# Strassen products for two row units in twelve gate/up pairs, silu as one ScalarE function, and another order in the first output pair

## The chip, the core and the metric

The kernel runs on one core of one Trainium2 chip. The metric is the device time of one execution in microseconds (us); less is better. A core has five engines with instruction queues of their own: TensorE (PE, with its weight loads as PEld), VectorE (DVE), ScalarE (ACT), GpSimd (POOL) and SyncE (SP), which here only issues DMAs. They wait for each other through semaphores.

## The reference, cut to what matters

Two layers of a decoder trunk on x of 256 rows by 2048 channels, all in float32. The part that this change bears on:

```python
for l in range(DEPTH):                       # 2
    h = rms_norm(x, mix_norm[l])
    proj = h @ w_in[l]                       # 2048 x 7680: q, k, v, u, v of the gating unit, two gates
    ...                                      # window attention, spatial gating, two branch projections
    merged = gates[..., :D_MODEL] * branch_a + gates[..., D_MODEL:] * branch_b
    x = x + merged @ w_out[l]                # 2048 x 2048
    h2 = rms_norm(x, ffn_norm[l])
    x = x + (jax.nn.silu(h2 @ w_gate[l]) * (h2 @ w_up[l])) @ w_down[l]   # 2048 x 5632, twice, and 5632 x 2048
```

## The kernel before, in words

**Products.** Every large matrix product is cut into weight tiles of 256 rows by 512 columns (a "half", 512 KB). A float32 weight tile `raw` is split into a high part `whi` (ScalarE, a copy to fp32r, line 228) and a low part `wlo = raw - whi` (VectorE, line 229); the activations, transposed, are kept as `uh` and `ul` in the same manner. One product of 128 rows of x with such a tile is six matmuls of 512 columns (`add_product`, lines 316 to 325): for each of two 128-row parts high by high, low by high, high by low. A "unit" is 512 channels of the activations, so two halves.

**The list of entries.** `plans` holds the work in order; a plan is one column block (`single`) or two column blocks that are worked together (`pair`): gate and up block f of the feed-forward part (key "ffn"), two blocks of w_out ("mix"), two of w_down ("hid"), two of w_in ("in"). All plans are flattened to one list `entries`. An entry with tag X, G or U takes one weight tile and both row blocks of x: two products. The entries with tags P1 to P7 are the seven products of a Strassen scheme (Winograd's form) over one unit and both column blocks, one product each, where the plain way takes four entries of two products. They need four weight tiles (k11, k12, k21, k22), four differences of them, made in place on VectorE (`sums`, line 213), four combinations of the activations (`sh`, `sl`, made by `sums` and `finished` in `transposed`, lines 467 to 482), and two results that are kept aside and given back (`kept`, lines 346 to 352). One unit of a pair is done so (unit `WINO` = 0); the others are plain. The first six entries of a pair (the head: P1, P5, P2, P6, P7, P4) are interleaved with the last six entries of the plan before, so that TensorE has plain work while ScalarE and VectorE copy between them; P3 stands in the body, behind the pair's third G entry.

**What runs ahead.** `Stream.next` is called once an entry: it asks for the weight DMAs of entries up to `W_LOAD` = 7 ahead (all on SP's queue), splits up to `W_SPLIT` = 4 ahead (four buffers each for `whi` and `wlo`, so that the split of entry n+4 waits until TensorE has done entry n), and makes the differences up to `W_SUM` = 6 ahead. Plain weight tiles rotate through five buffers; k11 to k22 have one each.

**Ticks.** Work that is not a weight split is queued with `after(n, fn)`, and `tick` counts once for every two products. `transposed` turns 512 channels by VectorE block transposes and 16 small DMAs (`turn`, lines 386 to 399; on POOL's queue, or half on SP's with `queue=None`), then makes the parts some ticks later; the tuples `WINO_...` give the ticks of the six steps for a unit that a Strassen scheme needs. With `on_pe` TensorE transposes instead (line 436).

**Order around the change.** In a layer: projections, attention and gating, the two branches with the gates (lines 933 to 952), two "mix" pairs with the residual (`residual`, line 867 on; the norm of the feed-forward part is made there), then three rounds of feed-forward: gate/up pairs 0 to 3, two "hid" pairs, pairs 4 to 7, two "hid" pairs, pairs 8 to 10, two "hid" pairs. `hidden` (line 961 on) makes one 512-channel block of the hidden layer: `on_gate` runs when the last G entry is done, `on_up` when the pair is done. Silu is made as x/2 times (1 + tanh(x/2)), with rhalf = r/2 and rr = r*r/2 from the norm: a ScalarE tanh (line 967), a VectorE product (line 968), and `on_up`'s product (line 972). The order on TensorE is that of the program; on the other engines a scheduler orders the instructions ahead of the launch.

Of the kernel before, what the change touches and what calls it, by code (L numbers as in the profile page):

```python
# [8 lines left out]
F32 = mybir.dt.float32  # L9
# [5 lines left out]
P = 128  # L15
# [42 lines left out]
def hybrid_trunk(ctx: ExitStack, tc: tile.TileContext, x, mix_norm, w_in, q_norm, k_norm, sinks,  # L58
# [62 lines left out]

        return Plan(key, [], [half(w, h, "X") for h in range(w.shape[0] // (2 * P))])

    def pair(key, wa, wb, by_unit=False):

        h1, h2 = 2 * WINO, 2 * WINO + 1
        l11, l12, l21, l22 = (load_of(w, h, t) for w, h, t in ((wa, h1, "k11"), (wb, h1, "k12"), (wa, h2, "k21"),  # L130
                                                              (wb, h2, "k22")))
        k11, k12, k21, k22 = l11[0], l12[0], l21[0], l22[0]
        rest = [h for h in range(wa.shape[0] // (2 * P)) if h // 2 != WINO]
        g, u = [half(wa, h, "G") for h in rest], [half(wb, h, "U") for h in rest]
        head = [dict(tag="P1", loads=[l11, l12], src=k11),
                dict(tag="P5", loads=[], sums=[(k11, k12, k11)], src=k11),
                dict(tag="P2", loads=[l21, l22], src=k21),
                dict(tag="P6", loads=[], sums=[(k11, k22, k11)], src=k11),
                dict(tag="P7", loads=[], sums=[(k12, k22, k12)], src=k12),
                dict(tag="P4", loads=[], sums=[(k21, k21, k11)], src=k21)]  # L140
        p3 = dict(tag="P3", loads=[], src=k22)
        body = g[:2] + [g[2], p3] + g[3:] + u
        g[1]["then"] = "open"
        if by_unit:
            body = g[:2] + [p3] + u[:2]
            g[0]["then"] = g[1].pop("then")
            for i in range(2, len(rest), 2):
                body += g[i:i + 2] + u[i:i + 2]
        return Plan(key, head, body)

    plans = []
    for l in range(DEPTH):
        wl = w_in[l]

        def of_in(kind, c):
            o = {"kv": O_KV, "q": 0, "v": O_V, "u": O_U, "gate": O_GATE}[kind] + c * CW
            return wl[:, o:o + CW]

        for f in FIRST_PART[l]:
            plans.append((single if len(f) == 1 else pair)(("in", l), *(of_in(*c) for c in f)))  # L160
        plans += [single(("att", l), w) for w in cols_of(w_attn_branch[l], NCH)]
        sgu = [single(("sgu", l), w_sgu_branch[l, :, j * CW:(j + 1) * CW]) for j in range(NCH)]
        plans += [sgu[0], pair(("in", l), of_in("gate", 5), of_in("gate", 6)), sgu[1], sgu[2],
                  single(("in", l), of_in("gate", 7)), sgu[3]]
        c_ = cols_of(w_out[l], NCH)
        plans += [pair(("mix", l), c_[j], c_[j + 1]) for j in range(0, NCH, 2)]
        for r, (f0, f1) in enumerate(ROUNDS):
            for f in range(f0, f1):
                plans.append(pair(("ffn", l), w_gate[l, :, f * CW:(f + 1) * CW], w_up[l, :, f * CW:(f + 1) * CW], f == 0))
            c_ = cols_of(w_down[l, f0 * CW:f1 * CW, :], NCH)  # L170
            plans += [pair(("hid", l, r), c_[j], c_[j + 1], j == 0) for j in range(0, NCH, 2)]
    entries = []
    for p in plans:
        if p.head:
            h, n = p.head, min(6, len(ahead.body))
            t = [entries.pop() for _ in range(n)][::-1]
            if n == 6:
# [3 lines left out]
            ahead_of = order[order.index(h[3]) - 1]  # L181
            ahead_of["loads"] = ahead_of["loads"] + h[2].pop("loads")
            h[2]["loads"] = []
            entries += order
        entries += p.body
        ahead = p

    class Stream:
# [7 lines left out]
        def load(self, upto):  # L196
            while self.asked < min(upto, len(entries)):
                for key, w, h, tag in entries[self.asked]["loads"]:
                    raw = wraw.tile([P, 2, CW], F32, tag=tag, name=nm("raw"), bufs=None if tag == "raw" else 1)
# [127 lines left out]
    def step():  # L327
# [4 lines left out]
        if tag in "XGU":  # L332
            ps = banks(p, "b" if tag == "U" else "a")
            todo = [(ps[t], block(units, e["h"], t)) for t in range(NT)]
        else:
            sh, sl = units[WINO][2:]
            which, t, form = {"P1": ("a", 1, (0, 0)), "P2": ("a", 0, (1, 0)), "P6": ("a", 1, 1), "P7": ("a", 1, 2),
                              "P4": ("a", 1, (1, 1)), "P5": ("a", 0, 0), "P3": ("b", 0, 3)}[tag]
            todo = [(banks(p, which)[t], (sh[:, form], sl[:, form]) if isinstance(form, int)
                     else block(units, 2 * WINO + form[0], form[1]))]  # L340
        for ps, u in todo:
            add_product(p, ps, u, w, tag in ("P4", "P7"))
        a, b = p.acc.get("a"), p.acc.get("b")
        if tag == "P5":
            p.kept = slot([P, 2, CW], name="kept")
            nc.scalar.activation(p.kept[:, 1, :], a[0], AF.Copy)
            nc.scalar.activation(a[0], a[1], AF.Copy)
        elif tag in ("P6", "P7"):
            nc.vector.tensor_tensor(out=p.kept[:, int(tag == "P7"), :], in0=a[1], in1=p.kept[:, 1, :], op=ALU.add)  # L349
# [144 lines left out]
    class Norm:  # L494
# [13 lines left out]
        def unit(self, c, on_pe=False, again=False, queue=nc.gpsimd, late=0):  # L508
            transposed(self.units, c, xs[:, :, c * CW:(c + 1) * CW], cols=self.cols[:, 4 * c:4 * c + 4],
                       on_pe=on_pe, again=again, queue=queue, late=late,  # L510
                       wino=None if c != WINO or on_pe else WINO_FIRST if again else WINO_IN if self.soon else
                       WINO_NORM)

        def finish(self):
            self.r, self.rh, self.rr = [], [], []
            for t in range(NT):
                v = tiny(1, f"var{t}", 2)
                nc.vector.tensor_reduce(out=v, in_=self.ss[t], axis=AX.X, op=ALU.add)
# [5 lines left out]
                rr = tiny(1, f"rr{t}", 2)  # L524
                nc.vector.tensor_tensor(out=rr, in0=r_, in1=rh, op=ALU.mult)
                self.r.append(r_)
                self.rh.append(rh)
                self.rr.append(rr)

    norm = Norm(first_cols)  # L530
    units_at["in", 0] = norm.units
# [335 lines left out]
    def residual(key, nxt=None, scale=1.0, store=False):  # L867

        def chunk(j, sums):
# [25 lines left out]
    for l in range(DEPTH):  # L895
# [43 lines left out]
        for j in range(NCH):  # L939
# [6 lines left out]
            for t in range(NT):  # L946
                nc.vector.scalar_tensor_tensor(out=gb[:, t, :], in0=gb[:, t, :], scalar=1.0, in1=ps[t],
                                               op0=ALU.add, op1=ALU.mult)
                nc.vector.tensor_tensor(out=ga[:, t, :], in0=ga[:, t, :], in1=gb[:, t, :], op=ALU.add)
# [11 lines left out]
        def hidden(hT, c):  # L961
            hid = slot([P, NT, CW], name="hid")

            def on_gate(g):
                for t in range(NT):
                    th = hid[:, t, :]
                    nc.scalar.activation(th, g[t], AF.Tanh, scale=norm.rh[t])  # L967
                    nc.vector.scalar_tensor_tensor(out=th, in0=th, scalar=1.0, in1=g[t], op0=ALU.add, op1=ALU.mult)  # L968

            def on_up(up):  # L970
                for t in range(NT):
                    nc.vector.scalar_tensor_tensor(out=hid[:, t, :], in0=up[t], scalar=norm.rr[t], in1=hid[:, t, :],
                                                   op0=ALU.mult, op1=ALU.mult)
                pe, soon = c == len(hT) - 1 == 2, c == 3
                after(3 if pe else 1 if soon else 2,
# [54 lines left out]
```

## Time and profile before

| what | us |
|---|---|
| median of 3 runs (2469.06 to 2469.82) | 2469.17 |
| the profiled execution's own time | 2468.67 |
| its span (first to last instruction) | 2467.0 |
| TensorE clock granted, mean | 0.999 |
| ScalarE busy / VectorE busy in the span | 1431.0 / 1932.5 |

The profiled execution's time is 1.67 us over its span, and 0.5 us under the median. A busy TensorE says only that matmuls followed each other; what one costs is read from the distance of their starts.

### The profile page before, as it was taken

What the parts mean: (1) busy time and instruction counts of PE and PEld (TensorE: products, weight loads), DVE (VectorE), ACT (ScalarE), POOL (GpSimd) and SP (SyncE); (2) the same over time, 40 slices, a digit from 0 to 9 for tenths busy, and PEclk for the clock granted to TensorE, in tenths of its full rate; (3) what the DMA queues carried; (4) which work ended last, traced back from release to release, by engine and by line L of the source; (5) the groups of instructions that cost most, each with busy time, mean ns of one, the idle gap of its engine ahead of it and who ended that gap; (6) DMA issues with size and microseconds to landing.
All of it is one profiled execution on the core that took longest, in us unless ns stands there. A gap on an engine that the chain in (4) does not pass through costs nothing.

```text
span 2467.0 us, 31322 instructions
## 1 busy us (share of the span) xinstructions
PE 2452.7 (99%) x11040; PEld 2027.6 (82%) x11040; DVE 1932.5 (78%) x2274; ACT 1431.0 (58%) x1793; POOL 309.3 (13%) x576
## 2 busy tenths in 40 slices
PE   9999999999999999999999999999999999999999
PEld 7888888888888888888887888888888888888887
DVE  6798676888877787778887986767888777877786
ACT  5567544565655565556655665455656555655564
POOL 3100002232110111001101000022311101110110
PEclk9999999999999999999999999999999999999999
DMA  9555667676666667576747446676767666666664
GB/s 293 199 187 162 214 197 220 184 235 205 216 210 202 216 193 234 180 225 190 225 153 265 154 154 225 205 213 182 236 198 233 200 216 195 219 207 203 215 195 146
DMA packets 279502, 505.69 MB, mean 205 GB/s; under 512 B 27760, under 2 KB 39120, under 8 KB 279344
## 3 DMA queue, kind: packets, MB, share of 16 engines
q1 hardware_dynamic: 261776, 485.83, 61.7%
q0 software_dynamic: 17248, 17.59, 2.7%
q8 instruction: 86, 1.41, 0.2%
q14 instruction: 72, 0.59, 0.1%
q10 hardware_dynamic: 320, 0.27, 0.0%
HBM read 475.27 MB, written 2.10 MB: 194 GB/s over the span
## 4 chain that ended last, share of the span: by engine, by line
PE 95%; DMA 2%; DVE 2%; SPq 1%; ACT 0%; issue 0%; POOL 0%; DVEq 0%; ACTq 0%
PE acc L324 61%; PE acc L325 31%; DMA raw<-in_w_in_dram 2%; DVE wlo L229 1%; PE po L780 1%; SPq L399 1%; PE psc L741 0%; PE ppt L770 0%; PE pt L436 0%; ACT whi L228 0%; PE psg L858 0%; POOL rq L296 0%; DVE box L393 0%; DVE ul L427 0%; DVE raw L213 0%
## 5 line engine op out<-in xcount | busy, mean ns | idle before, releaser
L229 DVE TENSOR_TENSOR wlo<-raw,whi 128x1024 fp32r<-128x1024 f32 (+1 forms) x1039 | 1261.8, 1220 | 478.8 <-ACT whi L228 465.7
L228 ACT ACTIVATE whi<-raw 128x1024 fp32r<-128x1024 f32 (+1 forms) x1038 | 1097.6, 1059 | 908.5 <-PE acc L325 709.9
L324 PE MATMUL acc<-whi,uh 128*128 128x512 f32 x3114 | 1216.6, 391 | 0.9 <-ACT uh L422 0.9
L324 PE MATMUL acc<-wlo,uh 128*128 128x512 f32 x3114 | 1213.3, 390 | 1.8 <-DVE wlo L229 1.8
L325 PE MATMUL acc<-whi,ul 128*128 128x512 f32 x3114 | 1212.8, 389 | 0.0
L324 PEld LDWEIGHTS acc<-wlo,uh 128*128 128x128 f32 x3114 | 585.2, 188 | 124.7 <-DVE wlo L229 4.2
L325 PEld LDWEIGHTS acc<-whi,ul 128*128 128x128 f32 x3114 | 585.0, 188 | 122.4 <-DVE ul L427 0.5
L324 PEld LDWEIGHTS acc<-whi,uh 128*128 128x128 f32 x3114 | 585.0, 188 | 121.7 <-ACT uh L422 1.1
L399 POOL DMA_DIRECT2D tt<-box x528 | 259.6, 499 | 1710.2 <-DMA raw<-in_w_up_dram 503.6
L213 DVE TENSOR_TENSOR raw<-raw,raw 128x1024 f32<-128x1024 f32 x188 | 229.4, 1220 | 1.3
L324 PE MATMUL acc<-whi,sh 128*128 128x512 f32 x376 | 147.2, 391 | 0.0
L324 PE MATMUL acc<-wlo,sh 128*128 128x512 f32 x376 | 146.9, 391 | 0.0
L325 PE MATMUL acc<-whi,sl 128*128 128x512 f32 x376 | 146.4, 389 | 0.0
L325 PEld LDWEIGHTS acc<-whi,sl 128*128 128x128 f32 x376 | 70.6, 188 | 14.8
L324 PEld LDWEIGHTS acc<-wlo,sh 128*128 128x128 f32 x376 | 70.6, 188 | 14.7 <-DVE kept L349 0.4
L324 PEld LDWEIGHTS acc<-whi,sh 128*128 128x128 f32 x376 | 70.6, 188 | 14.3
L349 DVE TENSOR_TENSOR kept<-acc,kept 128x512 f32<-128x512 f32 x94 | 64.3, 684 | 0.0
L352 ACT ACTIVATE acc<-kept 128x512 f32<-128x512 f32 x94 | 55.0, 586 | 11.0 <-DVE kept L349 10.9
L875 DVE SCALAR_TENSOR_TENSOR xs<-acc,xs 128x512 f32<-128x512 f32 (+1 forms) x66 | 41.4, 667 | 7.8 <-PE acc L325 7.8
L967 ACT ACTIVATE hid<-acc,rhalf 128x512 f32<-128x512 f32 x44 | 30.4, 690 | 20.7 <-PE acc L325 20.7
L419 DVE TENSOR_TENSOR ul<-tt,uh 128x512 fp32r<-128x512 f32 x52 | 34.0, 685 | 2.9 <-ACT uh L418 2.9
L968 DVE SCALAR_TENSOR_TENSOR hid<-hid,acc 128x512 f32<-128x512 f32 x44 | 29.6, 684 | 8.3 <-ACT hid L967 8.3
(137 smaller groups left out, 874.9 us busy)
## 6 DMA issues: line engine op xcount, KB each, us to landing
raw<-in_w_in_dram SPq DMA_DIRECT2D x239, 512.0 KB, 4.8
raw<-in_w_up_dram SPq DMA_DIRECT2D x176, 512.0 KB, 5.0
raw<-in_w_gate_dram SPq DMA_DIRECT2D x176, 512.0 KB, 4.3
raw<-in_w_down_dram SPq DMA_DIRECT2D x176, 512.0 KB, 5.0
raw<-in_w_out_dram SPq DMA_DIRECT2D x64, 512.0 KB, 5.1
tt<-box POOLq DMA_DIRECT2D x528, 32.0 KB, 4.4
raw<-in_w_attn_branch_dram SPq DMA_DIRECT2D x32, 512.0 KB, 5.5
raw<-in_w_sgu_branch_dram SPq DMA_DIRECT2D x32, 512.0 KB, 4.4
```

Of the source, the lines that this page charges most:

```text
L213: self.last = nc.vector.tensor_tensor(out=self.raws[d], in0=self.raws[x], in1=self.raws[y], op=ALU.subtract)
L228: self.high = nc.scalar.activation(hi[:, i, :], raw[:, i, :], AF.Copy)
L229: self.last = nc.vector.tensor_tensor(out=lo[:, i, :], in0=raw[:, i, :], in1=hi[:, i, :].bitcast(F32), op=ALU.subtract)
L324: nc.tensor.matmul(ps, a, part[:, kk, :], start=first and kk + n == 0, stop=False, skip_group_check=True)
L325: nc.tensor.matmul(ps, b, hi[:, kk, :], start=False, stop=kk == 1, skip_group_check=True)
L349: nc.vector.tensor_tensor(out=p.kept[:, int(tag == "P7"), :], in0=a[1], in1=p.kept[:, 1, :], op=ALU.add)
L352: nc.scalar.activation(ps, p.kept[:, t, :], AF.Copy)
L399: q.dma_start(dst[j * B:(j + 1) * B, i], box[i * B:(i + 1) * B, j])
L419: nc.vector.tensor_tensor(out=l, in0=s_, in1=h.bitcast(F32), op=ALU.subtract)
L875: nc.vector.scalar_tensor_tensor(out=xs[:, t, sl], in0=sums[t][:, i * w:(i + 1) * w], scalar=scale, in1=xs[:, t, sl], op0=ALU.mult, op1=AL ...
L967: nc.scalar.activation(th, g[t], AF.Tanh, scale=norm.rh[t])
L968: nc.vector.scalar_tensor_tensor(out=th, in0=th, scalar=1.0, in1=g[t], op0=ALU.add, op1=ALU.mult)
```

## The change

**Two units share banks.** `pair(..., two=True)` does units 0 and 1 by Strassen products: the products of both units with the same tag go to the same PSUM bank one after the other, and only behind the second one are results kept, copied or given back (`done`). It is used in the gate/up pairs 4, 5, 6, 8, 9 and 10 of each layer, twelve in all. Such a pair has a head of twelve entries, two P3 in the body, and four G and four U entries. The head is interleaved with nine entries of the plan before instead of six. Between two such pairs one period of the entry list then is (a and b are units 0 and 1; g and u are entries of two products, P of one):

```
g0 g1 P1a P1b g2 P3a P5a P5b P3b g3 P6a P6b P2a P2b u0 u1 P7a P7b u2 u3 P4a P4b
```

where g, u and P3 belong to one pair and the other P to the next. The loads of unit 1's four weight tiles take a slot of the general pool (25 buffers of 4 KB a partition) instead of buffers of their own, and those of both P2 are asked for with P5.

**Preparing unit 1.** Its four combinations are made once a layer, 24 ticks behind the last "mix" chunk, by a second call of `transposed` for that unit (again two block transposes, 16 DMAs, scaled copies, four sums, a split).

**Silu.** One ScalarE function `Silu` takes the place of tanh; the VectorE product of line 968 falls away, and `on_up` multiplies by r. `rr` is no longer made.

**First output pair.** With `last_later` its last two G entries stand behind the first two U entries; the last gate chunk is transposed one tick later; the ticks of the norm's unit 0 are two earlier, and its 16 DMAs go half by SP, half by POOL.

```diff
-WINO_NORM = 7, 8, 10, 11, 12, 13
+WINO_NORM = 5, 6, 8, 9, 10, 11
+W_TWO = 24
@@ pair
+        both = (WINO, WINO + 1) if two else (WINO,)
+        for w in both:
+            h1, h2 = 2 * w, 2 * w + 1
+            l11, l12, l21, l22 = (load_of(m, h, t if w == WINO else "slot")
+                                  for m, h, t in ((wa, h1, "k11"), (wb, h1, "k12"), (wa, h2, "k21"), (wb, h2, "k22")))
...
+            for e in head[-1] + p3[-1:]:
+                e["unit"], e["done"] = w, w == both[-1]
+        head = [e for es in zip(*head) for e in es]
...
-        body = g[:2] + [g[2], p3] + g[3:] + u
+        body = g[:3] + p3 + g[3:] + u
+        if last_later:
+            body = g[:3] + p3 + g[3:4] + u[:2] + g[4:] + u[2:]
@@ plans
-        plans += [pair(("mix", l), c_[j], c_[j + 1]) for j in range(0, NCH, 2)]
+        plans += [pair(("mix", l), c_[j], c_[j + 1], last_later=j == 0) for j in range(0, NCH, 2)]
+                                  two=r > 0 and f - f0 < 3))
@@ entries
-            h, n = p.head, min(6, len(ahead.body))
+            h, n = p.head, min(6 if len(p.head) == 6 else 9, len(ahead.body))
+            if n == 9:
+                order = t[:1] + h[:2] + t[1:3] + h[2:4] + t[3:5] + h[6:8] + h[4:6] + t[5:7] + h[8:10] + t[7:9] + h[10:]
+                for i in range(2):
+                    h[2 + i]["loads"], h[4 + i]["loads"] = h[4 + i]["loads"], []
@@ step
-        if tag == "P5":
+        if not e.get("done", True):
+            pass
+        elif tag == "P5":
@@ residual
-                after(1 if last else 2, lambda: nxt.unit(j, j > 0 and nxt.soon, queue=None if last else nc.gpsimd,
+                after(1 if last else 2, lambda: nxt.unit(j, j > 0 and nxt.soon, queue=None if last or j == WINO and not nxt.soon else nc.gpsimd,
+                    if not nxt.soon:
+                        after(W_TWO, lambda: nxt.unit(WINO + 1, again=True))
@@ gates
-            after(2 + (j == NCH - 1), lambda j=j, ga=ga: transposed(mT, j, ga, on_pe=j == NCH - 1,
+            after(2 + 2 * (j == NCH - 1), lambda j=j, ga=ga: transposed(mT, j, ga, on_pe=j == NCH - 1,
@@ hidden
-                    th = hid[:, t, :]
-                    nc.scalar.activation(th, g[t], AF.Tanh, scale=norm.rh[t])
-                    nc.vector.scalar_tensor_tensor(out=th, in0=th, scalar=1.0, in1=g[t], op0=ALU.add, op1=ALU.mult)
+                    nc.scalar.activation(hid[:, t, :], g[t], AF.Silu, scale=norm.r[t])
...
-                    nc.vector.scalar_tensor_tensor(out=hid[:, t, :], in0=up[t], scalar=norm.rr[t], in1=hid[:, t, :],
+                    nc.vector.scalar_tensor_tensor(out=hid[:, t, :], in0=up[t], scalar=norm.r[t], in1=hid[:, t, :],
```

More of the change, by code (lines that the diff above doesn't have):

```diff
@@ L122, in single, with pair @@
         return Plan(key, [], [half(w, h, "X") for h in range(w.shape[0] // (2 * P))])
[L124 to L133, printed above, removed]
-        g, u = [half(wa, h, "G") for h in rest], [half(wb, h, "U") for h in rest]
[L135 to L141, printed above, removed]
-        body = g[:2] + [g[2], p3] + g[3:] + u
+    def pair(key, wa, wb, by_unit=False, last_later=False, two=False):
+        head, p3 = [], []
+        both = (WINO, WINO + 1) if two else (WINO,)
[3 more added lines that the diff above has]
+                                  for m, h, t in ((wa, h1, "k11"), (wb, h1, "k12"), (wa, h2, "k21"), (wb, h2, "k22")))
+            k11, k12, k21, k22 = l11[0], l12[0], l21[0], l22[0]
+            head.append([dict(tag="P1", loads=[l11, l12], src=k11),
+                         dict(tag="P5", loads=[], sums=[(k11, k12, k11)], src=k11),
+                         dict(tag="P2", loads=[l21, l22], src=k21),
+                         dict(tag="P6", loads=[], sums=[(k11, k22, k11)], src=k11),
+                         dict(tag="P7", loads=[], sums=[(k12, k22, k12)], src=k12),
+                         dict(tag="P4", loads=[], sums=[(k21, k21, k11)], src=k21)])
+            p3.append(dict(tag="P3", loads=[], src=k22))
+            for e in head[-1] + p3[-1:]:
+                e["unit"], e["done"] = w, w == both[-1]
+        head = [e for es in zip(*head) for e in es]
+        rest = [h for h in range(wa.shape[0] // (2 * P)) if h // 2 not in both]
+        g, u = [half(wa, h, "G") for h in rest], [half(wb, h, "U") for h in rest]
+        body = g[:3] + p3 + g[3:] + u
@@ L180, in hybrid_trunk @@
                 order = [h[0], t[0], h[1], t[1], h[3], h[2], t[2], h[4], t[3], h[5]]
-            ahead_of = order[order.index(h[3]) - 1]
-            ahead_of["loads"] = ahead_of["loads"] + h[2].pop("loads")
-            h[2]["loads"] = []
+            if n != 9:
+                ahead_of = order[order.index(h[3]) - 1]
+                ahead_of["loads"] = ahead_of["loads"] + h[2]["loads"]
+                h[2]["loads"] = []
             entries += order
@@ L198, in load @@
                 for key, w, h, tag in entries[self.asked]["loads"]:
-                    raw = wraw.tile([P, 2, CW], F32, tag=tag, name=nm("raw"), bufs=None if tag == "raw" else 1)
+                    raw = (slot([P, 2, CW], name="raw") if tag == "slot" else
+                           wraw.tile([P, 2, CW], F32, tag=tag, name=nm("raw"), bufs=None if tag == "raw" else 1))
                     src = w[2 * h * P:2 * (h + 1) * P, :].rearrange("(k p) n -> p k n", p=P)
@@ L335, in step @@
         else:
-            sh, sl = units[WINO][2:]
             which, t, form = {"P1": ("a", 1, (0, 0)), "P2": ("a", 0, (1, 0)), "P6": ("a", 1, 1), "P7": ("a", 1, 2),
                               "P4": ("a", 1, (1, 1)), "P5": ("a", 0, 0), "P3": ("b", 0, 3)}[tag]
-            todo = [(banks(p, which)[t], (sh[:, form], sl[:, form]) if isinstance(form, int)
-                     else block(units, 2 * WINO + form[0], form[1]))]
+            todo = [(banks(p, which)[t], tuple(x[:, form] for x in units[e["unit"]][2:]) if isinstance(form, int)
+                     else block(units, 2 * e["unit"] + form[0], form[1]))]
         for ps, u in todo:
```

14 lines of the change are left out of this document (5 added, 9 removed).

## Prediction

> **What bounds the kernel now.** I read the page first, then the costliest groups, the waits and a stretch of the timeline.
>
> ```profile
> span 2467.0 us, 31322 instructions
> PE 2452.7 (99%) x11040; PEld 2027.6 (82%) x11040; DVE 1932.5 (78%) x2274; ACT 1431.0 (58%) x1793; POOL 309.3 (13%) x576
> PEclk9999999999999999999999999999999999999999
> PE 95%; DMA 2%; DVE 2%; SPq 1%; ACT 0%; issue 0%; POOL 0%; DVEq 0%; ACTq 0%
> ```
>
> The fourth line is the chain that ended last: 95% of it is TensorE, at full clock. So time falls if TensorE gets fewer matmuls, and rises where somebody lets it wait. The price of a matmul is the distance of starts, not the recorded 390 ns (they overlap). Six matmuls, one product, lie between these two rows of the timeline:
>
> ```profile
> 605.07 0.39 PE L324 MATMUL acc<-whi,uh 128*128 128x512 f32 x1
> 606.43 0.39 PE L324 MATMUL acc<-whi,uh 128*128 128x512 f32 x1
> ```
>
> One product is 1.36 us, a matmul 0.2267. The waits say who has kept TensorE, and what limits the engines that feed it:
>
> ```profile
> PE pt L436 <- DVE gate L949: 2.9, 2, 1.4
> PE acc L324 <- DVE wlo L229: 1.8, 5, 0.6
> ACT whi L228 <- PE acc L325: 709.9, 646, 4.4
> DVE wlo L229 <- ACT whi L228: 465.7, 486, 7.8
> ```
>
> (total us, times, longest.) TensorE waited 2.9 us for the transposes of the last gate chunk and 1.8 for low parts. The feeders wait in a ring: ScalarE for a buffer that TensorE must free, VectorE for ScalarE. They have slack, VectorE less.
>
> **The change part by part.**
>
> *Twelve units by seven products instead of eight.* One product saved in each of 12 pairs (2 layers, rounds of blocks 4 to 6 and 8 to 10): 12 x 1.36 = **16.3 us** off TensorE, since the granted clock and the form of the matmuls stay. Nothing is added on TensorE; results of both units are copied and kept once.
>
> *The gate chunk's transposes one tick later.* A tick is two products, 2.72 us, the wait is 1.4 each of two times; and last_later puts two U entries ahead of the G entries that read this chunk, 5.44 us. **-2.9 us**. What is late next is those G entries; behind the transposes stand P3, g3 and the two U entries, 9.5 us, for four short copies.
>
> *What the second unit costs its feeders.* Rows by form (busy us, mean ns):
>
> ```profile
> L229 DVE TENSOR_TENSOR wlo<-raw,whi 128x1024 fp32r<-128x1024 f32 x1035 | 1259.1, 1222 | 478.8 <-ACT whi L228 465.7 <-DMA raw<-in_w_up_dram 3.0 <-DMA tt<-box 1.5
> L213 DVE TENSOR_TENSOR raw<-raw,raw 128x1024 f32<-128x1024 f32 x188 | 229.4, 1220 | 1.3
> L349 DVE TENSOR_TENSOR kept<-acc,kept 128x512 f32<-128x512 f32 x94 | 64.3, 684 | 0.0
> L972 DVE SCALAR_TENSOR_TENSOR hid<-acc,rr,hid 128x512 f32<-128x512 f32 x44 | 30.9, 744 | 0.0
> L968 DVE SCALAR_TENSOR_TENSOR hid<-hid,acc 128x512 f32<-128x512 f32 x44 | 29.6, 684 | 8.3 <-ACT hid L967 8.3
> L393 DVE STREAM_TRANSPOSE box<-hid 128x512 f32<-128x512 f32 x40 | 28.2, 704 | 0.0
> L228 ACT ACTIVATE whi<-raw 128x1024 fp32r<-128x1024 f32 x1035 | 1095.8, 1060 | 908.5 <-PE acc L325 709.9 <-DVE raw L213 54.5 <-issue 52.5
> L967 ACT ACTIVATE hid<-acc,rhalf 128x512 f32<-128x512 f32 x44 | 30.4, 690 | 20.7 <-PE acc L325 20.7
> L467 ACT ACTIVATE sh<-sums 128x1024 fp32r<-128x1024 f32 x12 | 12.6, 1046 | 0.5 <-DVE sums L482 0.5
> L463 ACT ACTIVATE flat<-tt 128x256 f32<-128x256 f32 x32 | 10.6, 401 | 0.0
> L468 DVE TENSOR_TENSOR sl<-sums,sh 128x1024 fp32r<-128x1024 f32 x12 | 14.6, 1218 | 0.0
> L482 DVE TENSOR_TENSOR sums<-flat 128x256 f32<-128x256 f32 x24 | 10.0, 419 | 0.0
> ```
>
> Back to back, VectorE starts the next operation before the recorded end of the last:
>
> ```profile
> 1044.28 1.23 DVE L229 TENSOR_TENSOR wlo<-raw,whi 128x1024 fp32r<-128x1024 f32 x1 [1.46 <-ACT whi L228]
> 1045.42 1.22 DVE L213 TENSOR_TENSOR raw<-raw,raw 128x1024 f32<-128x1024 f32 x1
> 1046.56 0.68 DVE L349 TENSOR_TENSOR kept<-acc,kept 128x512 f32<-128x512 f32 x1
> 1047.16 2.35 DVE L229 TENSOR_TENSOR wlo<-raw,whi 128x1024 fp32r<-128x1024 f32 x2
> 1050.91 0.69 DVE L349 TENSOR_TENSOR kept<-acc,kept 128x512 f32<-128x512 f32 x1
> ```
>
> A 1024-wide one occupies 1.14 us, a 512-wide one 0.60. Between two two-unit pairs a period has 22 entries and 30 products, 40.8 us of TensorE. VectorE has 22 low parts and 8 differences, 30 x 1.14 = 34.2; two kept sums 1.2; two up products, 744 ns each and so some 0.66 apart, 1.3: 36.7. Such periods are 4 to 5 and 8 to 9 (call them A), and 5 to 6 and 9 to 10 (B), in two layers: eight in all. B has also the two block transposes of the round's first block, 1.3: 38.0. So VectorE is filled to 90 and 93%: no loss over the period, but its freedom is gone. Before, a period was 31 products, 42.2 us, with 23 x 1.14 + 1.2 + 1.2 (the product of L968) + 1.3 and, at most, some 2.5 for a hidden block: 32.4, 77%.
>
> Now the order inside. A high part starts 0.2 us after TensorE has freed the buffer of the entry four before (row below: 605.27 against 605.07), takes 1.06, the low part 1.14 more.
>
> ```profile
> 605.27 1.06 ACT L228 ACTIVATE whi<-raw 128x1024 fp32r<-128x1024 f32 x1 [1.66 <-PE acc L325]
> 606.63 0.69 ACT L967 ACTIVATE hid<-acc,rhalf 128x512 f32<-128x512 f32 x1 [0.30 <-PE acc L325]
> 607.99 0.69 ACT L967 ACTIVATE hid<-acc,rhalf 128x512 f32<-128x512 f32 x1 [0.67 <-PE acc L325]
> 608.58 1.05 ACT L228 ACTIVATE whi<-raw 128x1024 fp32r<-128x1024 f32 x1
> ```
>
> Counting from the start of g0, with each difference two entries ahead of its split, I get the low part of g3 at 15.6 us and TensorE there at 16.3; P6a 17.9 against 19.0, P6b 19.0 against 20.4, P2a 20.7 against 21.8. At g3's end ScalarE must wait for both banks for Silu (the rows at 606.63 and 607.99), so the high part of P2b runs from 20.1 to 21.1, its low part to 22.2, against 23.1. In B the scaled copies of the first hidden block (2 x 401 ns, some 0.65 together) come in there too: 0.3 to 0.5 us are left. Then u0 23.4 against 24.5, u1 26.2 against 27.2, P7a 28.9 against 29.9. Nothing is late, nothing by much more than 1 us in time. Bounds: nothing, to 1 us of stall in each of the eight, 8 us; nearest row is the 1.8 us that low parts cost all of before, so I take 0.2 each, **+1.6 us**.
>
> *Weights.* In such a period 11 of 16 tiles (5.8 MB) are asked for in some 14 us, 420 GB/s. The chip moved this much in two stretches:
>
> ```profile
> 10.00:30.00 20.00, 19.87 (x93) 16.19 (x92) 11.79 (x26) 13.16 (x29) 4.88 (x9) 0.92 1.05 373
> 295.00:305.00 10.00, 10.00 (x45) 8.27 (x45) 6.33 (x6) 5.75 (x7) 0.00 (x0) 1.00 1.04 388
> raw<-in_w_up_dram SPq DMA_DIRECT2D x176, 512.0 KB, 5.0
> ```
>
> (the last column of the first two is GB/s; the third is a tile's median us to landing.) At 388 they take 14.9, one us more than asked. k11 comes free with P4a's difference at about 32 us and must be back for the next high part at 39.4: 5.0 fits. I take 0; one of 512 KB late would cost about its 1.35 us of transfer, 8 times 11 at most in the eight.
>
> *The hidden block ahead of the last "hid" pairs.* The steps of a round's first hidden block are due at fixed ticks, and pair 10 is shorter in front of the next head: its P5 stood five products behind the last step (sh, sl) and now directly behind it, with g3's Silu in between. ScalarE needs 1.05, VectorE 1.14 more. If the scheduler puts sh ahead of the Silus, 0.7 us are lost; between them, 1.2; behind both, 2.9. I take 1.0 in each of two layers, **+2.0 us**; bounds 0 and 5.8.
>
> *Preparing unit 1.* Per layer on VectorE 2 x 0.70 + 4 x 0.42 + 1.22 = 4.3 us, on ScalarE 4 x 0.40 + 1.05 = 2.7, 16 small DMAs on POOL. It falls into round 0, whose stretch has 31 us of idle VectorE and 72 of ScalarE in 175, and POOL's queue 147:
>
> ```profile
> 585.00:760.00 175.00, 175.00 (x774) 144.96 (x773) 144.08 (x161) 103.08 (x115) 27.58 (x56) 1.00 0.69 218
> ```
>
> Cost 0; with that cover gone 2 x 7.0 = 14 us.
>
> *Silu.* The product of L968 goes (29.6 us), from an engine that has idled: 0 on the path, at most the 1.8 us above. The function itself I price as the tanh row, 690 ns. It may need another table:
>
> ```profile
> L272 ACT ACT_TABLE_LOAD x1 | 1.3, 1283 | 1.3 <-PEq L1008 1.3
> ```
>
> One load served copy, square, tanh and exp. If Silu lies elsewhere, three loads are added (into layer 0's feed-forward, out of it, into layer 1's): 3.85 us of ScalarE. Two meet wide entries with slack, the third the crowded start of layer 1. Bounds 0 and 3.85, I take half a load, **+0.6 us**. [...]
>
> *Order of the first output pair.* The last G two entries later and the ticks two earlier cancel: unit 0 of the norm is ready as before. Eight DMAs move to SP, ahead of weight loads. The chain has such an issue with its price:
>
> ```profile
> 109.70 0.59 SPq L399
> ```
>
> 8 x 0.59 = 4.7 us of SP, twice. Loads are asked for far enough ahead (five plain buffers, some 11 us less the 5.0 to landing); the same split is used before for the last chunk, and TensorE never waited there. 0; without the cover 9.4.
>
> **The sum.** -16.3 - 2.9 + 1.6 + 2.0 + 0.6 = -15.0. From the profiled execution's 2468.67 that is 2453.7; the median of before stands 0.5 above it, so **2454.2**.
>
> **The rivals.** *No stall at all:* 2468.67 - 19.2 + 0.5 = 2450.0. For it: TensorE waited 1.8 us for low parts in the whole of before. Faster as well.
>
> *The feeders eat it:* 1 us in each of eight periods, 2.9 in each of two layers and 3.85 for tables: 8 + 5.8 + 3.9 = 17.7 against 19.2, so 2467.7: within 0.2%. For it speaks B's slack of 0.3 us, against it the same row.
>
> *Table loads around each Silu:* if copy weren't in Silu's table, 88 loads, 113 us of ScalarE. A pair would have 2.6 us more in front of P2b; less the slack of about 1 that is 8 x 1.6 = 12.8, 2466 to 2467. Against it: copy, square, tanh and exp share one load. [...]
>
> *Slower: difference, high part and low part run one after the other.* In a head each product needs a difference (VectorE), then a high part (ScalarE), then a low part (VectorE). Were VectorE idle for the 1.06 us of each of the eight, a period would need 36.7 + 8.5 = 45.2 in A and 46.5 in B, against 40.8: 4.4 and 5.7 lost, four times each, 40 us; with the sum above less its 1.6, 2492.5. It decides from 3.0 us a period (24.1 / 8). Against it: the rows from 1044.28 to 1051.5, a head now, show VectorE waiting 0.3 us; for it, 12 one-product entries in a period instead of six or seven, and VectorE at 90%.
>
> **How the numbers follow.** About 0.2% (4.9 us) is what a measurement can tell from no change. Forecast 0.56, no stall 0.30, feeders 0.04, tables 0.02, serial 0.08. Faster 0.86, same 0.06, slower 0.08. The range goes from 2449.0 (no stall, and something of the 1.8 us) to 2465.0, where the stalls of the heads, of P5 and the tables are near their upper ends.
>
> **What would show it.** Matmuls of 512 columns fall by 72. The gate wait on L436 is gone. The waits of TensorE for wlo, sh and sl tell the 1.6 and the 2.0; they should stand at P2b in B and at the P5 behind pair 10. VectorE's share in A and B is 90% or more. Table loads are four. I am wrong if TensorE waits over 1 us in most of the eight heads, or for weight DMAs, or if loads stand beside each Silu.

## The result, and the profile after

The changed kernel takes 2457.38 us (median of 6 runs, 2456.94 to 2459.4), the kernel before 2469.11 beside it: ratio 0.9949, 95% interval 0.9939 to 0.9958, so 11.7 us less (10.4 to 15.1 by the interval) where 15.0 were forecast. The profiled execution took 2457.45 us, its span is 2455.7. From the page, as before:

```profile
span 2455.7 us, 31363 instructions
PE 2438.1 (99%) x10968; PEld 2012.6 (82%) x10968; DVE 1999.5 (81%) x2320; ACT 1472.5 (60%) x1842; POOL 315.6 (13%) x592
PE 90%; DVE 3%; DMA 3%; SPq 1%; issue 1%; ACT 1%; DVEq 0%; ACTq 0%
```

Matmuls fall from 11040 to 10968, the 72 that were counted. VectorE has 67 us more to do, ScalarE 42. In the last line, the chain that ended last, TensorE has fallen from 95% to 90%: the chain passes through the other engines more often. That is no measure of what was lost; TensorE's own waits are 13.5 us in all, 10.0 before. These lead (total us, times, longest):

```profile
PE acc L341 <- DVE sl L485: 3.2, 2, 1.6
PE acc L340 <- DVE wlo L245: 2.9, 5, 0.8
PE ppt L783 <- DVE wsT L654: 2.4, 1, 2.4
PE acc L340 <- ACT acc L364: 1.7, 1, 1.7
```

The wait for the gate chunk is gone. Two waits are new: for sl, twice (the low part of unit 0's combinations for the last "hid" pairs), and for the ScalarE copy that moves the kept banks (line 364), once.

The eight tight periods are not among them. Here are layer 0's: windows of 40.8 us that hold period A and B of round 1, then of round 2 (length; busy us and count of TensorE, weight loads, VectorE, ScalarE, POOL; granted clock, busy share of the DMA engines, GB/s):

```profile
806.50:847.30 40.80, 40.80 (x181) 33.78 (x180) 37.19 (x35) 25.38 (x28) 0.00 (x0) 1.00 0.56 180
847.30:888.10 40.80, 40.80 (x181) 33.78 (x180) 38.47 (x37) 27.78 (x34) 7.84 (x16) 1.00 0.61 192
1055.80:1096.60 40.80, 40.80 (x181) 33.78 (x180) 37.19 (x35) 25.38 (x28) 0.00 (x0) 1.00 0.55 179
1096.60:1137.40 40.80, 40.80 (x181) 33.56 (x180) 37.87 (x37) 27.63 (x34) 7.86 (x16) 1.00 0.63 192
```

Each holds 180 matmuls in 40.8 us, 0.2267 apiece (the 181st lies across an edge): TensorE loses nothing while VectorE is busy for 91 to 94%.

The loss is just behind them, where the head of the last "hid" pairs begins. TensorE, then VectorE, from the timeline:

```profile
1153.22 0.40 PE L340 MATMUL acc<-wlo,sh 128*128 128x512 f32 x1
1155.19 0.50 PE L341 MATMUL acc<-whi,sl 128*128 128x512 f32 x1 [1.58 <-DVE sl L485]
```

```profile
1151.31 0.42 DVE L499 TENSOR_TENSOR sums<-flat,sums 128x256 f32<-128x256 f32 x1
1151.65 1.22 DVE L245 TENSOR_TENSOR wlo<-raw,whi 128x1024 fp32r<-128x1024 f32 x1
1152.78 1.22 DVE L229 TENSOR_TENSOR raw<-raw,raw 128x1024 f32<-128x1024 f32 x1
1153.92 1.22 DVE L485 TENSOR_TENSOR sl<-sums,sh 128x1024 fp32r<-128x1024 f32 x1
```

P5's third matmul is due 0.23 us behind the second and starts 1.97 behind it. With the smaller delays around it the place costs 2.1 us, in both layers. The last sum of the combination ends at 1151.7, and a low part and a difference for later weights stand between it and sl. In layer 1 a second stall follows, at P6. ScalarE's timeline there:

```profile
2381.04 1.06 ACT L244 ACTIVATE whi<-raw 128x1024 fp32r<-128x1024 f32 x1 [1.67 <-PE acc L341]
2382.01 1.13 ACT L435 ACTIVATE uh<-tt 128x512 fp32r<-128x512 f32 x2
2383.05 0.57 ACT L363 ACTIVATE kept<-acc 128x512 f32<-128x512 f32 x1
2383.76 1.06 ACT L244 ACTIVATE whi<-raw 128x1024 fp32r<-128x1024 f32 x1
2384.73 0.58 ACT L364 ACTIVATE acc<-acc 128x512 f32<-128x512 f32 x1
```

P5 has been done since about 2378.3, but its two copies (lines 363 and 364) stand behind a high part that waits for a later entry, behind two parts of another hidden block and behind one more high part. P6 has to wait for the second copy until 2385.3.

### The profile page after: what moved, and what is told of

Its sections match the earlier page's. It is cut to its first block, busy times and chain, and to the rows that moved or that the text cites. A ratio compares the mean times of both kernels' runs of the same rounds, so it can differ in the third digit from the quotient of the medians.

```text
span 2455.7 us, 31363 instructions
## 1 busy us (share of the span) xinstructions
PE 2438.1 (99%) x10968; PEld 2012.6 (82%) x10968; DVE 1999.5 (81%) x2320; ACT 1472.5 (60%) x1842; POOL 315.6 (13%) x592
## 4 chain that ended last, share of the span: by engine, by line
PE 90%; DVE 3%; DMA 3%; SPq 1%; issue 1%; ACT 1%; DVEq 0%; ACTq 0%
PE acc L340 59%; PE acc L341 29%; DMA raw<-in_w_in_dram 2%; DVE wlo L245 2%; SPq L416 1%; ACT whi L244 1%; PE po L793 1%; PE psc L754 0%; PE ppt L783 0%; DVE raw L229 0%; PE psg L871 0%; PE pt L453 0%; DMA raw<-in_w_up_dram 0%; DMA raw<-in_w_down_dram 0%; DVE box L410 0%
## 5 line engine op out<-in xcount | busy, mean ns | idle before, releaser
L244 ACT ACTIVATE whi<-raw 128x1024 fp32r<-128x1024 f32 (+1 forms) x1074 | 1132.0, 1059 | 883.0 <-PE acc L341 623.4
L245 DVE TENSOR_TENSOR wlo<-raw,whi 128x1024 fp32r<-128x1024 f32 (+1 forms) x1075 | 1301.3, 1219 | 399.0 <-ACT whi L244 386.7
L340 PE MATMUL acc<-whi,uh 128*128 128x512 f32 x2994 | 1170.3, 391 | 1.2 <-ACT uh L439 1.2
L340 PE MATMUL acc<-wlo,uh 128*128 128x512 f32 x2994 | 1167.1, 390 | 3.0 <-DVE wlo L245 2.9
L341 PE MATMUL acc<-whi,ul 128*128 128x512 f32 x2994 | 1166.4, 390 | 0.0
L229 DVE TENSOR_TENSOR raw<-raw,raw 128x1024 f32<-128x1024 f32 x236 | 287.8, 1219 | 1.6 <-DMA raw<-in_w_up_dram 0.8
L341 PE MATMUL acc<-whi,sl 128*128 128x512 f32 x472 | 184.0, 390 | 3.2 <-DVE sl L485 3.2
L340 PE MATMUL acc<-whi,sh 128*128 128x512 f32 x472 | 184.8, 392 | 1.7 <-ACT acc L364 1.7
L340 PE MATMUL acc<-wlo,sh 128*128 128x512 f32 x472 | 184.2, 390 | 0.0
L435 ACT ACTIVATE uh<-tt 128x512 fp32r<-128x512 f32 x52 | 29.8, 618 | 9.4 <-DMA tt<-box 9.4
```

Of the source, the lines that this page charges most:

```text
L229: self.last = nc.vector.tensor_tensor(out=self.raws[d], in0=self.raws[x], in1=self.raws[y], op=ALU.subtract)
L244: self.high = nc.scalar.activation(hi[:, i, :], raw[:, i, :], AF.Copy)
L245: self.last = nc.vector.tensor_tensor(out=lo[:, i, :], in0=raw[:, i, :], in1=hi[:, i, :].bitcast(F32), op=ALU.subtract)
L340: nc.tensor.matmul(ps, a, part[:, kk, :], start=first and kk + n == 0, stop=False, skip_group_check=True)
L341: nc.tensor.matmul(ps, b, hi[:, kk, :], start=False, stop=kk == 1, skip_group_check=True)
L435: nc.scalar.activation(h, s_, AF.Copy)
```

## The experiments

Twelve kernels were run, each with the kernel before on the same chip. "Stretch" below is what the distances between neighbouring 512-wide matmuls have over 0.2267 us in the profiled execution, summed where it is more than 15 ns: 10.9 us before, 19.6 after. The waits are always TensorE's.

**One part alone.** First the order of the first output pair, without the rest.

```diff
-WINO_NORM = 7, 8, 10, 11, 12, 13
+WINO_NORM = 5, 6, 8, 9, 10, 11
...
+        if last_later:
+            body = g[:3] + [p3] + g[3:4] + u[:2] + g[4:] + u[2:]
...
-            after(2 + (j == NCH - 1), lambda j=j, ga=ga: transposed(mT, j, ga, on_pe=j == NCH - 1,
+            after(2 + 2 * (j == NCH - 1), lambda j=j, ga=ga: transposed(mT, j, ga, on_pe=j == NCH - 1,
```

The call with `last_later=j == 0` and the queue of the norm's unit 0 are changed as well.

> The kernel before with only the other order of the first output pair (last G entries later, gate transposes one tick later, the norm's unit 0 two ticks earlier with its DMAs on two queues). Theory: the two waits of 1.4 us for the gate chunk go and nothing else moves, 2.9 us less than before. Rival (the freed time is lost at the next wait, the parts of the first unit or the loads behind eight more DMAs on SP's queue): within 0.7 us of before, with new waits of TensorE between 460 and 600 us of the span.

Ratio 0.9985 (0.9977 to 0.9994), 3.7 us with an interval of 1.5 to 5.7. The wait for the gate chunk is gone, none has come between 460 and 600 us. As the theory said. Then everything but the two units:

```diff
-                                  two=r > 0 and f - f0 < 3))
+                                  two=False))
```

> The changed kernel with two=False: Silu, the other order of the first output pair and the preparation of unit 1 stay, all pairs have one Strassen unit. Theory (the two units give 16.3 us on TensorE and take back 6 to 7 in stalls of their own; the rest is worth 2.9): 2466 to 2467, no wait of TensorE for sl or for the copies of kept banks, matmuls back by 72. Rival (the stalls come from Silu's table loads or from the preparation of unit 1): the stalls of 2 us at the last hid pairs stay and the time is above 2469.

Ratio 0.9988 (0.9979 to 0.9997), 3.0 us less than before; no wait for sl or copies. So the two units are worth the difference of 0.9949 and 0.9988, some 9.6 us of the 16.3 that they take off TensorE (each ratio is known to some 2 us); about 7 go to what they bring with them. Silu and the preparation of unit 1, which this kernel has over the one before it, together show neither gain nor loss.

**Silu undone.**

```diff
-                    nc.scalar.activation(hid[:, t, :], g[t], AF.Silu, scale=norm.r[t])
+                    nc.scalar.activation(th, g[t], AF.Tanh, scale=norm.rh[t])
+                    nc.vector.scalar_tensor_tensor(out=th, in0=th, scalar=1.0, in1=g[t], op0=ALU.add, op1=ALU.mult)
...
-                    nc.vector.scalar_tensor_tensor(out=hid[:, t, :], in0=up[t], scalar=norm.r[t], in1=hid[:, t, :],
+                    nc.vector.scalar_tensor_tensor(out=hid[:, t, :], in0=up[t], scalar=norm.rr[t], in1=hid[:, t, :],
```

> The changed kernel with silu as tanh and a VectorE product again: two 512-wide VectorE operations (1.2 us) more in each of 44 pairs, no added table loads. Theory (VectorE has about 1 us of freedom at the crowded place of the eight periods between two-unit pairs, P2b, and these operations fall on it): up to 0.8 us in each, so 1 to 6 us slower than the changed kernel, 2458 to 2463, with TensorE waiting for wlo at P2b. Rival (Silu's relief is off the path altogether): within 0.7 us of 2457.4.

(A layer has 11 gate/up pairs, so there are 22; 44 are the operations, two a pair, 26 us in all.) Ratio 0.9950 (0.9937 to 0.9962), equal to the changed kernel. The time is the rival's, but this run doesn't decide: the distances of matmuls are stretched in five new places in the gate/up rounds, by 0.2 to 1.0 us each and 2.5 in all, and in this build the late copy, 1.9 us, has not come up. The two offset each other. The same edit without that copy follows further down.

**The stall for sl.** The steps of the hidden block due two ticks earlier:

```diff
-WINO_HID = 7, 8, 17, 18, 19, 20
+WINO_HID = 7, 8, 15, 16, 17, 18
```

> The changed kernel, with the last four steps of the hidden block's unit 0 due two ticks (5.4 us) earlier. Theory (the stall at the P5 behind pair 10 is a matter of the due time alone): TensorE's waits for sl (3.2 us, two times) go, the trace has some 4 us less of stretched distances between matmuls, and the time falls by 4 us to about 2453.4. Rival (VectorE is too full in that stretch, so that whatever is moved makes something else late): the waits for sl shrink, others for wlo or kept results appear in the same two places or in the heads of pairs 6 and 10, and the time stays within 1 us of 2457.4.

Ratio 0.9963 (0.9950 to 0.9975): not faster than the changed kernel. Its five executions run from 2457.89 us, at a mean granted clock of 0.999, to 2465.88, at 0.995; the last section offers a reason. The wait for sl is gone, but

```profile
PE acc L340 <- ACT acc L364: 6.7, 2, 3.3
```

the copies are now late in both layers, by 3.3 us. So the due time was not all. The rival is right in that something else became late, but VectorE's fill was not the reason: the new wait is for ScalarE, whose queue in this build has two high parts and the two parts of pair 9's hidden block ahead of the copies. I formed another theory: the price lies in the order in which two engines' queues have been laid out. The two parts (uh) are due one tick behind P5; moved away, they should let the copies through.

```diff
-                                         queue=None if soon else nc.gpsimd, late=-2 if soon else 0))
+                                         queue=None if soon else nc.gpsimd, late=-2 if soon else 2 if c == 1 and len(hT) == 3 else 0))
```

> The changed kernel with only the two parts of the second hidden block two ticks later in the last round. Theory: the copies of the kept banks are no longer late (1.8 us, once), the stalls for sl (2.1 us, two times) stay; about 2 us less. Rival (the copies were late for another reason): the wait for them stays.

The wait for the copies is gone, the two for sl stay. ScalarE in the place shown above:

```profile
2377.21 0.60 ACT L363 ACTIVATE kept<-acc 128x512 f32<-128x512 f32 x1 [1.26 <-PE acc L341]
2377.70 1.05 ACT L244 ACTIVATE whi<-raw 128x1024 fp32r<-128x1024 f32 x1
2378.65 0.59 ACT L364 ACTIVATE acc<-acc 128x512 f32<-128x512 f32 x1
2379.93 1.06 ACT L244 ACTIVATE whi<-raw 128x1024 fp32r<-128x1024 f32 x1 [0.69 <-PE acc L341]
2380.90 1.13 ACT L435 ACTIVATE uh<-tt 128x512 fp32r<-128x512 f32 x2
```

The copies now start with P5's end and the parts come behind. The stretch falls by 3.8 us, to 15.8. Of this 1.9 are the copies; 1.7 are matmuls at half speed at the start of layer 1, which the changed kernel's profile has (last section) and this one hasn't: its mean granted clock is 1.000, so the clock costs it 0.0005 x 2453 = 1.2 us at most in all. No run shows that these 1.7 are the edit's doing; TensorE's wait for wsT in that place is 2.6 us here and 2.4 in the changed kernel. The times don't resolve 1.9 us (0.9949, 0.9937 to 0.9962). Both edits together (this kernel is the base of what follows; where a recorded expectation speaks of both ticks moved, it is meant):

> The changed kernel with the last four steps of the hidden block's unit 0 two ticks earlier, as in the first of these runs, and, in the last round, the two parts of the second hidden block two ticks later, so that they no longer stand on ScalarE's queue around the copies of the kept banks. Theory (the loss behind pair 10 is the order of two engines' queues: VectorE's for sl, ScalarE's for the copies): both stalls go, 6 us less than the changed kernel, some 2451.5 where before has 2469.1, ratio 0.993. Rival (whatever is moved there makes something else late): within 2 us of the changed kernel, with another wait of TensorE at the same place.

Ratio 0.9929 (0.9916 to 0.9941): 17.5 us less than before, about 5 less than the changed kernel. Neither wait is left; the stretch is 14.5.

**How full VectorE may be.** Four more VectorE sums in each two-unit head:

```diff
+        if len(p.head) == 12 and e.get("done") and tag in ("P1", "P6"):
+            for _ in range(2):
+                nc.vector.tensor_tensor(out=temp(name="extra"), in0=xs[:, 0, :CW], in1=xs[:, 1, :CW], op=ALU.add)
```

> The changed kernel with four more 512-wide VectorE sums (0.60 us each, their results unused) in each two-unit head, two behind unit 1's P1 and two behind unit 1's P6: 2.4 us more VectorE work in each of twelve heads, 29 us in all. Theory (VectorE's 90 to 93% in the eight tight periods leaves 2.8 to 4.1 us free, of which about 1 us can be used at the crowded place): most of it is hidden, TensorE's waits for wlo grow by 0.2 to 0.8 us a tight period, 2 to 6 us in all. Rival (VectorE is the bound of these periods already): every added microsecond is paid, 20 us or more.

Ratio 1.0014 (1.0005 to 1.0023), 16 us over the changed kernel, near what the rival asks. But the profile says otherwise than either:

```profile
752.33 2.49 DVE L361 TENSOR_TENSOR extra<-xs 128x512 f32<-128x512 f32 x4
```

The sums read x alone, so they could run long before, and the twelve sums of all three heads of a round were drawn into one place (751 to 765 us here), ahead of the first; there TensorE lost 3.5 us over kept results and low parts, in each of the four rounds. That is no answer to how full a period may be. The second dose ties each sum to its own head and stands on the kernel without the two stalls (the edit against the first dose):

```diff
-                nc.vector.tensor_tensor(out=temp(name="extra"), in0=xs[:, 0, :CW], in1=xs[:, 1, :CW], op=ALU.add)
+                nc.vector.tensor_tensor(out=temp(name="extra"), in0=w[1][:, 0, :].bitcast(F32),
+                                        in1=w[1][:, 1, :].bitcast(F32), op=ALU.add)
```

> The run of the seventh kind (early and late: ratio 0.9929) with four more 512-wide VectorE sums in each two-unit head, as in the dose run, but each reads the low part that was just made, so that it can't be drawn together with those of other heads and must be done before that buffer is used again; their results are unused. 2.4 us more VectorE work in each of twelve heads. Theory (the earlier dose cost 15 us because twelve of them were put in one place; in their own head the tight periods hide most of 2.4 us): TensorE's waits for wlo and kept results grow by at most 0.5 us a head, 6 us in all, ratio below 0.9955. Rival (VectorE is the bound of the two-unit periods): 2 us or more a head, 20 us and more, ratio above 1.0.

Ratio 0.9938 (0.9924 to 0.9951), 2.2 us over its base by the ratios, whose intervals overlap, for 29 us of added work. The two periods of round 1 in layer 0, in windows of 41 us:

```profile
806.00:847.00 41.00, 41.00 (x182) 33.95 (x182) 39.30 (x38) 25.21 (x28) 0.00 (x0) 1.00 0.59 176
847.00:888.00 41.00, 40.58 (x178) 33.06 (x178) 40.10 (x41) 28.31 (x36) 7.86 (x16) 1.00 0.62 188
```

A hides it all, VectorE at 96%; B, at 98%, loses 0.42 us. In layer 1 the same B loses 0.74 and 0.45, more than the 0.5 a head that I allowed; over all heads the waits for low parts are 2.4 us. The theory holds in the main: VectorE is not the bound of these periods. Silu undone on the same base, 1.2 us in each of the 22 pairs:

> The run of the seventh kind with silu as tanh and a VectorE product: 1.2 us more VectorE work in each of 44 pairs. Theory (VectorE's relief by Silu is nearly all off the path): waits for wlo grow by 0 to 3 us in all, ratio 0.993 to 0.994. Rival (it is what makes two units possible at all): 6 us or more, ratio above 0.9953.

Ratio 0.9926 (0.9913 to 0.9938): no loss to be seen, and no new wait above 0.33 us in the pairs. Silu's relief of VectorE is off the path.

**Two units more.** Pair 7 too:

```diff
-                                  two=r > 0 and f - f0 < 3))
+                                  two=r > 0))
```

> The changed kernel with two units in every pair of rounds 1 and 2, so pair 7 too: fourteen instead of twelve pairs, 12 matmuls fewer, 2.7 us of TensorE. Theory (the price of a two-unit head is small and lies in single places, not in VectorE's fill): 1.5 to 2.7 us less than the changed kernel, ratio to before 0.9940 or so. Rival (four tight heads in a row drain what the feeders had in hand): new waits for wlo in period 6 to 7, nothing gained or slower.

Ratio 1.0001 (0.9992 to 1.0010): 2.7 us less work on TensorE, and 13 us slower than the changed kernel. Neither of the two accounts: it is not VectorE, it is the copies again.

```profile
PE acc L340 <- ACT acc L364: 12.7, 4, 4.4
PE acc L340 <- DVE wlo L245: 3.8, 8, 0.6
```

The profiled execution is 16.0 us over the changed kernel's. In it the waits for copies are 11.0 us longer, and the mean granted clock is 0.996 against 0.999, which by my estimate is some 7 us (0.003 x 2472; 5 to 10, as the means are rounded).

So I laid the order down: on the base with both ticks moved, what follows a copy in the program is queued behind it on ScalarE.

```diff
-            nc.scalar.activation(a[0], a[1], AF.Copy)
+            stream.copied = nc.scalar.activation(a[0], a[1], AF.Copy)
...
+                            with tc.issue_after(self.copied.ins):
+                                self.high = nc.scalar.activation(hi[:, i, :], raw[:, i, :], AF.Copy)
...
-            with tc.issue_after(stream.last.ins):
+            with tc.issue_after(stream.last.ins), tc.issue_after((stream.copied or stream.last).ins):
                 fn()
```

With twelve pairs:

> The run of the seventh kind, with the high parts and the ticks' work on ScalarE queued behind the copies of the kept banks that precede them in the program. Theory (nothing is left that the order of the copies costs at twelve pairs): same as that run, ratio 0.993, no wait of TensorE for the copies. Rival (the forced order makes ScalarE wait for P5 where it had work): waits for wlo grow, 2 us or more slower.

Ratio 0.9925 (0.9913 to 0.9938), as its base; no wait for copies. With fourteen:

> The forced order of the run beside it, and two units in every pair of rounds 1 and 2: fourteen pairs, 2.7 us less TensorE work. Theory (the loss of 13 us with fourteen pairs was the order of ScalarE's queue, four late copies of 3.3 to 4.5 us and what followed them): the waits for the copies go, and the time is 1 to 3 us below that of the run beside it. Rival (four tight heads in a row drain VectorE's and ScalarE's lead): waits for wlo of 1 us and more in the periods 6 to 7, slower than the run beside it.

Ratio **0.9911** (0.9897 to 0.9925), 2449.4 us: 22 us less than before and the lowest median of all. It is 2.9 us under the twelve pairs' 2452.34; the intervals overlap. No copy is waited for any more. The leading waits of twelve pairs, then of fourteen:

```profile
PE ppt L788 <- DVE wsT L659: 3.2, 1, 3.2
PE acc L345 <- DVE wlo L250: 1.4, 6, 0.5
```

```profile
PE acc L345 <- DVE wlo L250: 5.6, 11, 1.3
PE pw L658 <- ACT pT L790: 1.5, 1, 1.5
```

So the loss of fourteen pairs came from the order of the queues, ScalarE's copies above all, and what followed from it. How much the moved ticks and how much the forced order took away isn't shown: fourteen pairs with the ticks alone were not run. Nor is it shown that the two added units pay by themselves. They save 2.7 us of matmuls; the waits for low parts are 4.2 us longer (1.1 of it in the periods from pair 6 to 7, as the rival had it, but below its 1 us each), at the start of layer 1 a wait of 3.2 us has given way to one of 1.5, and the mean granted clock is 1.000 against 0.998, by my estimate some 5 us (0.002 x 2450; 2 to 7, as the means are rounded).

## Why the prediction was right, point by point

*16.3 us off TensorE, 2.9 of the gate wait*: both as said, the first to the matmul; the second also alone.

*Eight tight periods, +1.6*: nothing lost in layer 0's four windows above, and no wait of TensorE falls into layer 1's either; the two small ones nearby (0.33 us each with the delay behind, at 919 and 2141) are at the last P4 ahead of pair 7. The fill was right: 36.7 and 38.0 us were worked out, 37.2 and 37.9 to 38.5 are shown. So was its meaning: the tied dose shows that 2.4 us more fit nearly free. The 0.2 us each that I took for them came to nothing in all eight. The rivals by which VectorE or its chain with ScalarE eats the gain are refuted by the same windows.

*P5 behind pair 10, +2.0*: the right place, mis-sized: 2.1 us in each of two layers, 4.2 in all. I let sl wait for ScalarE's sh and Silu; in fact sh was placed ahead of Silu and ready at 1152.8, the case that I had priced at 0.7, and VectorE's queue had a difference for other weights in front of sl, 1.1 us more.

*The copies, 1.9 us*: not in the sum. I had priced copies by their cover on TensorE (three or four products) and never asked what stands ahead of them on ScalarE.

*Table loads, +0.6*: nothing. Three were added, the one that I had feared falls into a stretch in which ScalarE waits anyway:

```profile
1327.92 1.28 ACT L771 ACT_TABLE_LOAD   x1
1330.97 0.40 ACT L771 ACTIVATE pr<-pr,negm 128x128 f32<-128x128 f32 x1 [1.76 <-DVE negm L764]
```

In front of the first Silu of a layer a load of 1.28 us stands alone, and the Silu starts 0.02 us behind its end:

```profile
575.77 1.28 ACT L981 ACT_TABLE_LOAD   x1 [0.34 <-PE acc L341]
577.07 1.27 ACT L981 ACTIVATE hid<-acc,rstd 128x512 f32<-128x512 f32 x2
```

The rival of loads around each Silu falls: there are four loads in all, 1.28 us each (L288 one, L771 one, L981 two for its 44 Silus), and copies run between the Silus without one. (Its 88 loads should have been 44: the two Silus of each of the 22 pairs stand together.)

*Weights, unit 1, the order of the first pair at 0*: no new wait of TensorE for any of them.

The sum of what was seen: -16.3 - 2.9 + 0.7 (wlo) + 4.2 (sl) + 1.9 (copies) + 1.7 (matmuls at half speed, last section) + 0.5 (a weight tile late at layer 1's start, 1.1 against 0.6 before) = -10.2, against a span shorter by 11.3. Matmul by matmul, the changed kernel is already 0.6 us ahead at 434 us, where no part of the change has come, and 0.3 are gained behind the last matmul; 0.2 stay unexplained.

That the total came so near is luck in part. Two terms that I had added, 2.2 us together, did not come; 2.2 us more at P5, the copies and the half speed did, and the last two were not in the sum.

## What to carry to other kernels

Here an engine filled to 91 to 98% cost next to nothing, and the waits came from single results that stood in a queue behind work for later. So when work is added or due times move, list for each result that the bound engine needs what stands ahead of it on its producer's queue, copies between banks too, and pin the order where a scheduler lays it. A dose of work put in to measure slack must depend on the place where it is meant to stand.

## What the runs showed of the hardware

Some waits of TensorE cost more than their length in these traces: the matmuls behind them ran at half speed for a while. In the changed kernel's profile, behind the 2.43 us wait for wsT at the start of layer 1:

```profile
1346.50 0.63 PE L340 MATMUL acc<-whi,uh 128*128 128x512 f32 x1
1346.93 0.63 PE L340 MATMUL acc<-wlo,uh 128*128 128x512 f32 x1
1347.36 0.63 PE L341 MATMUL acc<-whi,ul 128*128 128x512 f32 x1
```

They start 0.43 us apart instead of 0.227; the ten distances from 1345.44 to 1349.40 take 3.96 us instead of 2.27, so 1.7 us are lost. The granted clock is 0.50 here (columns as in the first section, the granted clock behind POOL):

```profile
1346.00:1349.00 3.00, 3.00 (x8) 2.32 (x7) 3.00 (x4) 1.36 (x3) 0.00 (x0) 0.50 0.72 259
```

In the kernel before, the wait for wsT in the same place was 2.33 us, and behind it TensorE ran on at a granted clock of 1.00, 0.227 us a matmul:

```profile
1352.23 0.66 PE L770 MATMUL ppt<-ident,pr 128*128 128x128 f32 x4 [2.33 <-DVE wsT L641]
1353.20:1356.20 3.00, 3.00 (x15) 2.49 (x14) 3.00 (x4) 1.90 (x4) 0.00 (x0) 1.00 0.73 265
```

The wait for sl in layer 1 is 1.58 us both in the tanh kernel and in the changed kernel. Behind it the tanh kernel's clock is 0.52, the changed kernel's 1.00:

```profile
2380.20 0.50 PE L341 MATMUL acc<-whi,sl 128*128 128x512 f32 x1 [1.58 <-DVE sl L485]
2380.60:2383.80 3.20, 3.20 (x10) 2.47 (x9) 2.64 (x4) 1.85 (x3) 0.00 (x0) 0.52 0.34 127
```

```profile
2377.03 0.50 PE L341 MATMUL acc<-whi,sl 128*128 128x512 f32 x1 [1.58 <-DVE sl L485]
2377.43:2380.63 3.20, 3.20 (x16) 2.63 (x15) 2.05 (x3) 1.06 (x1) 0.00 (x0) 1.00 0.30 111
```

So in these four places the length of the wait does not tell whether half speed follows: it did behind 2.43 and behind 1.58 us, and it did not behind 2.33 and behind another 1.58. What else decides is not shown, and no run shows that the 1.7 us come from the change.

The traced execution of the first run on sl has such a stretch too, behind the late copy in layer 0, which ended at 1163.72:

```profile
1165.00:1168.20 3.20, 3.20 (x9) 2.45 (x9) 2.11 (x3) 1.06 (x1) 0.00 (x0) 0.50 0.89 307
```

The five executions of that run differ by 8.0 us, and their mean granted clock falls from 0.999 to 0.995 with it. By my estimate the clock alone is then worth 0.004 x 2460 = 9.8 us (7 to 12, as the means are rounded), which would cover the difference; only one of the five was traced.
